# Reads of scratch and states moved to GpSimd's queue, with a new head, RMS step and end, in a one-core decoder layer

## The chip, the core and the metric

The kernel runs on one NeuronCore of a Trainium2 chip. Its engines work in parallel and meet through semaphores: TensorE (PE, matmuls; its weight loads are shown as PEld), VectorE (DVE), ScalarE (ACT), GpSimd (POOL) and SyncE (SP, which here only issues DMAs). Each engine takes its instructions strictly in order. A DMA is issued by an engine's queue and carried out by 16 shared DMA engines; SyncE and GpSimd issue them here. The metric is device time in microseconds (us); less is better.

## The reference

One inference step of one layer (DEPTH = 1), all in float32, for a prompt of 256 tokens and 8 samples of 8 tokens each (320 tokens, D_MODEL = 2048), with shared weights:

```
mod = silu(c) @ w_ada + b_ada                      # six vectors of 2048 per sequence: shift, scale, gate, twice
h   = rms_norm(x) * (1 + scale_m) + shift_m
z   = h @ w_in                                     # RWKV columns (3328), gMLP u, v (1024 each), gate logits (2 x 2048)
o_a = rwkv7(token_shift(z_rwkv), states)           # per head: S <- S diag(w) - (S kk)(a kk)^T + v k^T, in 16 heads of 64
y_a = o_a @ w_branch_a
y_b = (gelu(u) * (W_s @ layer_norm(gelu(v)) + b)) @ w_branch_b      # mixing in chunks of 128 positions
x   = x + gate_m * ((sigmoid(g_a) * y_a + sigmoid(g_b) * y_b) @ w_out)
h2  = rms_norm(x) * (1 + scale_f) + shift_f
x   = x + gate_f * ((silu(h2 @ w_gate) * (h2 @ w_up)) @ w_ffn_out)  # D_FF = 5632
y   = rms_norm(x)
```

Outputs are y of both groups, the new RWKV states and shift buffers of both, and the normalised gMLP v rows of the samples.

## The kernel before

The 320 tokens are the moving columns of every matmul and channels lie on partitions. A product in float32 is made of three matmuls with operands split into a high and a low part (`mms`, lines 174 to 176: high x high, low x high, high x low). Weights come as tiles `ws` of up to 1 MB (`wload`, line 162; `wf` in the FFN, line 1289) into three buffers; ScalarE copies the high part (`wh`) and VectorE subtracts it for the low part (`wl`), each in four buffers. So a weight tile is on the way, waits to be split, or is split, and TensorE works on the split parts in the order in which the program was written, as a scheduler placed it on each engine before the run.

The stages, in order of time:

- **Head** (0 to about 200 us). `x_stats` squares x in four quarters (two buffers `sq`), sums them with a matmul against ones (line 366) and takes root and reciprocal (`rst`). `ada_half` and `ada_cols` load columns of w_ada (tiles `wa`, lines 279 and 306) and multiply them with silu(c) (lines 281, 317); w_in's first 26 column tiles follow as soon as a stretch of h is modulated (`h_mod`), into `zx`.
- **Preparation** (about 200 to 400 us). Per pair of heads j, `prep1` to `prep3` build the recurrence's operands and store them in DRAM scratch: `d_w` (line 753), `d_kc` (754), `d_l` (763). The gate logits of w_in are worked off between them by `fill(n)`, which takes n units from a list of matmul units, and stored in `d_sg` (`g_evict`, line 548, four buffers `sg`).
- **Samples** (about 400 to 560 us). `chunk_load(4)` reads M, KB, v, Q and KC back (lines 824 to 843), `solve_load` reads the triangular systems (778, 780), `sample_t` the transposed states `s0t` (984, two buffers), `state_load` the states `s0` (971, three buffers) and the decays `dp` (1000). `sample_keys` has GpSimd and VectorE make the key products `we`; `sample_state` (line 1020) multiplies, adds and stores the new state (1022).
- **Prompt chunks** (about 560 to 750 us). Four chunks of 64 tokens, each with `chunk_load`, `chunk_g`, `chunk_w`, `chunk_t` (Tc and Lc, lines 884 and 889), `chunk_x`, `chunk_o`, `chunk_s` and `chunk_n` (factors `gb`, line 950; stores `d_o`).
- **Branches** (about 740 to 880 us). `read_split` (553) reads the two branch inputs back; w_branch_b and w_branch_a follow with their gate tiles `gt` read by `ahead_of` (562, six buffers of each kind). Branch b's gated result goes to `d_mb` (569) and is read again for branch a.
- **w_out and the RMS step** (about 880 to 1030 us). `o_evict` adds to the residual `xr` and sums squares in `acc`; `token_sums` (1236) makes sums per token, `rn2` the reciprocal roots, `dg` diagonals, and a matmul with ones (1266) spreads them to all partitions for h2 (`h2h`, `h2l`).
- **FFN** (about 1030 to 1975 us) and the **end**: the last RMS norm, a product with `rf` in seven parts (`y`), each part stored by SyncE (1356).

The modulation columns of groups 2 to 5 are a list `adas` of 17 units a group (16 loads of 1 MB, with a batch of 16 matmuls at every second one, and a flush). `fill` takes from it at a rate per unit until 17 are left, which are group 5's; the RMS step takes three of these and the FFN the rest.

All stores, the parameter rows and the residual's x are issued by GpSimd (`sd = nc.gpsimd.dma_start`); everything else, that is weights, modulation columns and all reads of scratch and states, by SyncE (`ld = nc.sync.dma_start`).

Of the kernel before, what the change touches and what calls it, by code (L numbers as in the profile page):

```python
# [42 lines left out]
F_C = [4, 2, 2, 3, 2, 3, 2, 2]  # L43
NIA, NB1, NB2 = 2, 1, 2
F_S = [1, 8, 2, 2, 6, 8, 2, 1]
# [29 lines left out]
def body(ctx, tc, I, O):  # L75
# [192 lines left out]
    def ada_half(k0, nk):  # L268

        w, kb, box = nk * 256, 8 // nk, {}  # L270

        def load(q):
            if q == 0:
                box["pa"] = ps_ax(512)
            a = 4 * q % kb
            if a == 0:
                box["wt"] = st.tile([128, kb, w], F32, tag="wa", name="wa", bufs=2)
            wt = box["wt"][:, a:a + 4]
            ld(wt, w_ada.block(4 * q, 4, (k0 * 128, nk * 128), (D + k0 * 128, nk * 128)))
# [18 lines left out]
        return [lambda q=q: load(q) for q in range(4)] + [flush]  # L298

    def ada_cols(pool, kb, c0s, w, dsts, kr=1, bufs=2):  # L300

        box, held = {}, []

        def load(kq):
            wt = (pool or late["w"])().tile([128, kb, 4 * w], F32, tag="wa", name="wa", bufs=bufs)
            ld(wt, w_ada.block(kq * kb, kb, *[(c0, 4 * w // len(c0s)) for c0 in c0s]))
            held.append((kq, wt))
# [23 lines left out]
    def ada_seg(k0, nk):  # L331
        if nk < 4:
            return ada_half(k0, nk)

        def dsts(pt):
            for gi in range(2):
                c = BADA + gi * KT + k0
                tt(mod[:, gi, k0:k0 + 4].rearrange("p (jj b) s -> p b jj s", b=2), pt[:, :, 2 * gi:2 * gi + 2, 0:9],
                   bct(par1[:, c:c + 4].rearrange("p (jj b) -> p b jj", b=2), 9), ADD)
            scale_of(amix, 1, GMIX, k0, 4)  # L340

        return ada_cols(lambda: st, 2, [k0 * 128, D + k0 * 128], 256, dsts)

# [49 lines left out]
    with tc.manual_schedule(engines={mybir.EngineType.Activation, mybir.EngineType.DVE, mybir.EngineType.PE}):  # L393
# [10 lines left out]
        rst2 = st.tile([128, T], F32, name="rst2")  # L404
        V.tensor_copy(rst2, rst)
    rst = rst2
    def rows2():
        sd(par2, I["par2"])
        sd(psh, I["state_shift"])


    units, avail = deque(), [SEGS[0][1]]
    for si, (k0, nk) in enumerate(SEGS[1:]):
# [11 lines left out]
        if si == 2:  # L425
            u.insert(0, params2)
        units.extend((f, RA[si]) for f in u)
# [340 lines left out]
    def solve_load():  # L768
# [49 lines left out]
    def chunk_load(c):  # L818
# [4 lines left out]
        for h, lo in ((0, 0), (1, 64)):  # L823
            ld(b["M"][lo:lo + 64, :, h], d_w[lo:lo + 64, c, :, 0:2].rearrange("p j q t -> p j (q t)"))
        ld(b["KB"][0:64], d_w[0:64, c, :, 2:4])
        for q in range(2):
            ld(b["KB"][64:128, :, q], d_w[64:128, c, :, 3 - q])

        for a in range(2):
            for h in range(2):  # L830
                ld(b["v"][64 * a:64 * a + 64, :, 1 - h], d_w[64 * h:64 * h + 64, c, a::2, 4])
        if c == 4:

            b["Q"] = cp.tile([128, NJ, 2, 2, 4, 2, TS], F32, name="Q2", tag="Q2")
            for a in range(2):
                for h in range(2):
                    ld(b["Q"][64 * a:64 * a + 64, :, h].rearrange("p j q a s t -> p j (q a s t)"), d_w[64 * h:64 * h + 64, 4, :, 0:2].rearrange("p j q t -> p j (q t)"))
# [3 lines left out]
            ld(b["KC"][0:64], d_kc[0:64])  # L841
            for q in range(2):
                ld(b["KC"][64:128, :, q], d_kc[64:128, :, 1 - q])
        cur[c] = b
# [36 lines left out]
    def chunk_t(c):  # L881
        b = cur[c]
        b["T"] = cp.tile([128, NJ, 64], F32, name="Tc", tag="Tc", bufs=nb)
        ld(b["T"], d_t[c].rearrange("j p t -> p j t"))
        if c == 4:
            return

        T, L = b["T"], cp.tile([128, NJ, 64], F32, name="Lc", tag="Lc", bufs=1)
        ld(L, d_l[c].rearrange("j p t -> p j t"))
        pt = ps_ax(NJ, 32)  # L890
# [78 lines left out]
    def load_s0(j):  # L969
        s0 = cm.tile([128, NS, 64], F32, name="s0", tag="s0", bufs=3)  # L970
        ld(s0, I["s0"][j])
        return s0
# [8 lines left out]
    def sample_t(j):  # L981

        s0t = cm.tile([128, 4, 128], F32, name="s0t", tag="s0t", bufs=2)
        ld(s0t, I["s0t"][j])
        return s0t
# [245 lines left out]
    def token_sums():  # L1231

        pn = ps_ax(3)
        for c, n in enumerate(rows):
            for q, a in enumerate((acc, fin["q"])):
                PE.matmul(pn[0:n, c:c + 1], a[:, c * 128:c * 128 + n], ones[:, 0:1], start=q == 0, stop=q == 1)
        return pn
# [17 lines left out]
    dg = p2.tile([128, T], F32, name="dg")  # L1255
# [4 lines left out]
    for c, n in enumerate(rows):  # L1260
        fin["d"] = V.tensor_scalar(dg[0:n, c * 128:c * 128 + n], ident[0:n, 0:n], rn2[0:n, c:c + 1], None, op0=MUL)
    for _ in range(NB2):
        adas.popleft()()
    rB = ps_ax(T)
    for c, n in enumerate(rows):
        PE.matmul(rB[:, c * 128:c * 128 + n], ones[0:n], dg[0:n, c * 128:c * 128 + n], start=True, stop=True)
    h2h = hp.tile([128, KT, T], F32R, name="h2h", tag="hh")
# [78 lines left out]

    pf = ps_ax(T)
    for q, a in enumerate((acc, fin["q"])):
        PE.matmul(pf, ones, a, start=q == 0, stop=q == 1)
    rf = p2.tile([128, T], F32, name="rf", tag="sq2", bufs=2)  # L1350
# [9 lines left out]
_OUTS = {"y": (128, KT, T), "wkv_p": (2, 64, NJ, 64), "shift": (128, 9, NRW), "wkv_s": (NJ, 128, NS, 64), "v": (NS * TS, 1024)}  # L1360

# [56 lines left out]
```

## Time and profile before

| | |
|---|---|
| time, median of 3 runs (lowest, highest) | 1992.02 us (1989.43, 1995.13) |
| profiled execution, its span | 1994.61 us, 1992.9 us |
| TensorE busy; mean granted clock | 1931.9 us (97%); 0.986 |
| VectorE, ScalarE, GpSimd busy | 1079.7, 763.2, 119.3 us |
| DMA moved | 420.89 MB, 211 GB/s over the span |

The span runs from the first to the last instruction of the profiled execution; its time has a little around it. Matmuls are pipelined and their ends are modelled, so a busy TensorE can still be at less than its best pace. A DMA-issuing instruction counts as busy time on GpSimd and not on SyncE.

### The profile page before, as it was taken

The page shows a single profiled execution, that of the slowest core. Times are in us where ns is not written, and L with a number is a line of the kernel's source. Part 1 is how long each engine was busy: PE and PEld are TensorE (multiplying, and loading weights), DVE is VectorE, ACT ScalarE, POOL GpSimd, SP SyncE. Part 2 cuts the span into 40 slices and gives each one's busy share as a digit, 9 for nine tenths or more (in the row PEclk, how much of TensorE's full clock was granted, in tenths as well). Part 3 has the DMA queues.
Part 4 walks back from the last instruction along what each step waited for, and adds up shares of the span by engine and source line. Part 5 has one row for each costly group of instructions (what it writes and reads, how often), then busy time and mean ns, then how long its engine had stood idle before and what let it go on. Part 6 is the DMA issues. An engine that isn't in the chain of part 4 may idle for free.

```text
span 1992.9 us, 34504 instructions
## 1 busy us (share of the span) xinstructions
PE 1931.9 (97%) x14213; PEld 1807.8 (91%) x14213; DVE 1079.7 (54%) x1902; ACT 763.2 (38%) x1095; POOL 119.3 (6%) x221
## 2 busy tenths in 40 slices
PE   6999999989999999899999999999999999999996
PEld 4788999979886898888889999999999999999996
DVE  5666677759655564464464335345454445345446
ACT  5333377534333334342244232333333333332333
POOL 1000112330310011000000000000000000000000
PEclk9999999989999999999989999999999999999998
DMA  7877446785798789888746753544535544453441
GB/s 295 312 303 302 153 157 253 258 212 188 218 259 267 236 322 317 301 308 346 296 166 221 258 180 117 159 159 142 164 129 159 159 159 130 153 173 127 149 169 74
DMA packets 132813, 420.89 MB, mean 211 GB/s; under 512 B 41872, under 2 KB 65424, under 8 KB 103728
## 3 DMA queue, kind: packets, MB, share of 16 engines
q1 hardware_dynamic: 124256, 388.19, 57.7%
q0 software_dynamic: 8400, 30.50, 4.3%
q8 instruction: 112, 1.84, 0.4%
q14 instruction: 45, 0.37, 0.1%
HBM read 390.40 MB, written 28.23 MB: 210 GB/s over the span
## 4 chain that ended last, share of the span: by engine, by line
PE 79%; issue 12%; DMA 3%; DVE 2%; POOL 2%; ACT 1%; SPq 0%; DVEq 0%; POOLq 0%; ACTq 0%
PE mm L174 25%; PE mm L175 24%; PE mm L176 24%; PE ax L317 2%; DMA gt<-d_sg 1%; PE ax L281 1%; DMA d_mb<-gt 1%; POOL d_sg L548 0%; DMA d_w<-pk 0%; DVE wl L98 0%; ACT wh L101 0%; DMA KB<-d_w 0%; DMA dp<-d_pe 0%; POOL we L98 0%; DMA par<-in_par 0%
## 5 line engine op out<-in xcount | busy, mean ns | idle before, releaser
L98 DVE TENSOR_TENSOR wl<-ws,wh 128x1024 fp32r<-128x1024 f32 (+1 forms) x304 | 362.4, 1212 | 284.8 <-ACT wh L101 284.5
L101 ACT ACTIVATE wh<-ws 128x1024 fp32r<-128x1024 f32 (+1 forms) x304 | 305.8, 1041 | 458.1 <-PE mm L175 346.7
L174 PE MATMUL mm<-h2h,wh 128*128 128x320 f32 x1408 | 436.4, 310 | 2.1 <-ACT h2h L101 2.1
L175 PE MATMUL mm<-h2l,wh 128*128 128x320 f32 x1408 | 435.9, 310 | 0.0
L176 PE MATMUL mm<-h2h,wl 128*128 128x320 f32 x1408 | 435.6, 310 | 0.0
L98 DVE TENSOR_TENSOR wl<-wf,wh 128x1024 fp32r<-128x1024 f32 x176 | 215.2, 1225 | 327.3 <-ACT wh L101 322.7
L174 PE MATMUL mm<-hh,wh 128*128 128x320 f32 x1184 | 376.9, 321 | 2.6 <-ACT wh L101 2.6
L176 PE MATMUL mm<-hh,wl 128*128 128x320 f32 x1184 | 369.4, 313 | 1.8 <-DVE wl L98 1.7
L175 PE MATMUL mm<-hl,wh 128*128 128x320 f32 x1184 | 370.2, 313 | 0.3 <-DVE hl L98 0.3
L101 ACT ACTIVATE wh<-wf 128x1024 fp32r<-128x1024 f32 x176 | 185.2, 1058 | 383.2 <-PE mm L175 358.2
L174 PEld LDWEIGHTS mm<-h2h,wh 128*128 128x128 f32 x1408 | 265.0, 188 | 8.1 <-issue 2.5
L175 PEld LDWEIGHTS mm<-h2l,wh 128*128 128x128 f32 x1408 | 265.1, 188 | 0.0
L176 PEld LDWEIGHTS mm<-h2h,wl 128*128 128x128 f32 x1408 | 265.0, 188 | 0.0
L174 PEld LDWEIGHTS mm<-hh,wh 128*128 128x128 f32 x1184 | 224.7, 191 | 28.1 <-issue 16.6
L175 PEld LDWEIGHTS mm<-hl,wh 128*128 128x128 f32 x1184 | 225.5, 190 | 6.1 <-issue 2.5
L176 PEld LDWEIGHTS mm<-hh,wl 128*128 128x128 f32 x1184 | 225.0, 190 | 6.1 <-DVE wl L98 3.4
L175 PE MATMUL mm<-fl,wh 128*128 128x320 f32 x704 | 216.5, 308 | 0.0
L174 PE MATMUL mm<-fh,wh 128*128 128x320 f32 x704 | 216.4, 307 | 0.0
L176 PE MATMUL mm<-fh,wl 128*128 128x320 f32 x704 | 216.3, 308 | 0.0
L176 PEld LDWEIGHTS mm<-fh,wl 128*128 128x128 f32 x704 | 131.9, 187 | 0.1
L174 PEld LDWEIGHTS mm<-fh,wh 128*128 128x128 f32 x704 | 131.9, 187 | 0.0
L175 PEld LDWEIGHTS mm<-fl,wh 128*128 128x128 f32 x704 | 131.9, 187 | 0.0
(322 smaller groups left out, 2144.5 us busy)
## 6 DMA issues: line engine op xcount, KB each, us to landing
wa<-in_w_ada SPq DMA_DIRECT2D x88, 1024.0 KB, 6.6
wf<-in_w_ffn_in SPq DMA_DIRECT2D x176, 512.0 KB, 3.5
ws<-in_w_in SPq DMA_DIRECT2D x64, 1024.0 KB, 6.6
ws<-in_w_ffn_out SPq DMA_DIRECT2D x40, 1024.0 KB, 4.8
ws<-in_w_out SPq DMA_DIRECT2D x16, 1024.0 KB, 7.1
d_w<-pk POOLq DMA_DIRECT2D x8, 1120.0 KB, 6.1
wa<-in_w_ada SPq DMA_DIRECT2D x16, 512.0 KB, 5.0
ws<-in_w_branch_b SPq DMA_DIRECT2D x8, 1024.0 KB, 6.1
```

Source lines behind the costliest of these rows:

```text
L98: return (eng or V).tensor_tensor(out, a, b, op=op)
L101: return A.activation(out, in_, fn, **kw)
L174: PE.matmul(ps, hi[:, k, sl], xh[:, kx + a + k], start=f, stop=False)
L175: PE.matmul(ps, hi[:, k, sl], xl[:, kx + a + k], start=False, stop=False)
L176: PE.matmul(ps, lo[:, k, sl], xh[:, kx + a + k], start=False, stop=e)
L281: PE.matmul(box["pa"][32 * j:32 * j + 32, 0:w], cT[:, 4 * q + j], wt[:, j], start=q == 0, stop=q == 3, tile_position=(0, 32 * j))
L317: PE.matmul(box["pa"][32 * j:32 * j + 32, 0:w], cT[:, k], wt[:, kk, j * w:j * w + w], start=kq == kr - 1 and q == kq and kk == 0, stop=kq ...
```

## The change

1. Reads of scratch and of recurrent states are issued by GpSimd: every `ld` of lines 553, 562, 778, 780, 824 to 843, 884, 889, 950, 971, 984 and 1000 becomes `sd`. SyncE keeps weights, modulation columns, the head's x and the final stores.
2. Head: the squares of x are written into `zx` (unused until then) in four places; the tiles `wa` get a third buffer; `params2` is put behind the head on VectorE.
3. RMS step: sums per token in three full groups of 128 (the last two overlap by 64 tokens) with one root and one reciprocal; a batch of group 5's modulation matmuls ahead of the sums, one between sums and spreading, one behind it. Its first four loads are issued by GpSimd during w_out, into buffers of the FFN that are still free.
4. End: sums per token as in the RMS step; y is turned on TensorE in 12 groups of four 128 x 128 transposes, scaled per token while it is copied out of PSUM by ScalarE and VectorE in turn, and stored in 12 parts with another layout of the output, which the host turns back.

```
-    sq = st.tile([128, 4, T], F32, name="sq", tag="sq", bufs=2)          # x_stats
+    sq = zx[:, 4 * q:4 * q + 4, 0:T]
-    box["wt"] = st.tile([128, kb, w], F32, tag="wa", name="wa", bufs=2)   # ada_half; ada_seg's ada_cols too
+    box["wt"] = st.tile([128, kb, w], F32, tag="wa", name="wa", bufs=3)
-        V.tensor_copy(rst2, rst)
+        headed = V.tensor_copy(rst2, rst)
+    def late_params2():
+        with tc.issue_after(headed.ins):
+            params2()
...
-            ld(um, src[:, j])                                             # read_split
+            sd(um, src[:, j])
-                ld(got[n, i], src[i])                                     # ahead_of
+                sd(got[n, i], src[i])
-            ld(b["M"][lo:lo + 64, :, h], d_w[lo:lo + 64, c, :, 0:2]...)   # chunk_load; KB, v, Q, KC likewise
+            sd(b["M"][lo:lo + 64, :, h], d_w[lo:lo + 64, c, :, 0:2]...)
...
+    def ada_ahead():
+        for kq in range(4):
+            t = p2.tile([128, FCH[0][1], T], F32R, name="wb", tag=("fh", "fl")[kq % 2], bufs=2)
+            wt = early[5 * D, kq] = t.rearrange(...)
+            sd(wt, w_ada.block(kq, 1, (5 * D, D)))                         # ada_cols' load takes it from early
...
+    fill(24)
+    ada_ahead()
     while main_q:
         fill(1)
-    while len(adas) > 15 + NB1:                                           # NB1 = 1
+    while len(adas) > 15:
         adas.popleft()()
     pn = token_sums()
-    for n, c0, c1 in ((128, 0, 2), (64, 2, 3)):
-        fin["a"] = act(rn2[0:n, c0:c1], pn[0:n, c0:c1], AF.Sqrt, scale=1.0 / D, bias=eps6[0:n])
-        V.reciprocal(rn2[0:n, c0:c1], rn2[0:n, c0:c1])
+    fin["a"] = act(rn2, pn, AF.Sqrt, scale=1.0 / D, bias=eps6)
+    V.reciprocal(rn2, rn2)
...                                                                        # dg, then two units of adas, as before
     rB = ps_ax(T)
-        PE.matmul(rB[:, c * 128:c * 128 + n], ones[0:n], dg[0:n, c * 128:c * 128 + n], start=True, stop=True)
+        PE.matmul(rB[:, t0:t0 + 128], ones, dg[:, c], start=True, stop=True)
+    for _ in range(2):
+        adas.popleft()()
...
-    act(rf, pf, AF.Sqrt, scale=1.0 / D, bias=eps6)                        # the end
-    V.reciprocal(rf, rf)
-    for k0, nk, eng in ((0, 1, V), (11, 2, G), (1, 2, V), (3, 2, V), (5, 3, V), (13, 3, G), (8, 3, V)):
-        o = y[:, k0:k0 + nk]
-        tt(o, o, rf.unsqueeze(1).to_broadcast([128, nk, T]), MUL, eng)
-        ld(O["y"][:, k0:k0 + nk], o)
+    def turned(c, q):
+        pt = ps_ax(4, 128)
+        t0 = (0, 128, T - 128)[c]
+        for k in range(4):
+            PE.transpose(pt[:, k], y[:, 4 * q + k, t0:t0 + 128], ident)
+        return pt.rearrange("p k t -> p (k t)")
+    first = [(0, 0), (0, 1), (0, 2)]
+    ahead = [turned(*cq) for cq in first]
+    pf = token_sums()
...
+    for n, (c, q) in enumerate(first + [(1, 0), (1, 1), (1, 2), (0, 3), (1, 3)] + [(2, q) for q in range(4)]):
+        pt = ahead[n] if n < len(ahead) else turned(c, q)
+        p0 = 64 if c == 2 else 0
+        o = ...
+        if n % 2:
+            V.tensor_scalar(o, pt[p0:], rf[p0:, c:c + 1], None, op0=MUL)
+        else:
+            act(o, pt[p0:], AF.Copy, scale=rf[p0:, c:c + 1])
+        ld(O["y"][c, q, 0:128 - p0], o)
```

## Rows read from the trace of the kernel before

**Rows 1.** Busy us (instructions) of PE, PEld, DVE, ACT, POOL; PEclk, DMA share, GB/s, by stretch.

```profile
404.00:416.00 12.00, 7.32 (x36) 6.75 (x34) 3.70 (x2) 1.84 (x2) 7.03 (x16) 0.72 1.11 237
436.00:450.00 14.00, 9.19 (x75) 8.50 (x74) 10.82 (x33) 4.01 (x4) 4.25 (x8) 0.76 0.83 292
524.00:560.00 36.00, 33.94 (x248) 25.67 (x247) 26.91 (x43) 10.59 (x15) 13.38 (x18) 0.98 0.74 238
560.00:750.00 190.00, 183.94 (x1959) 157.18 (x1958) 105.18 (x127) 68.68 (x103) 13.87 (x22) 0.98 0.85 270
750.00:875.00 125.00, 117.60 (x802) 105.88 (x801) 59.21 (x91) 51.51 (x85) 10.22 (x19) 1.00 0.87 311
1019.00:1034.00 15.00, 11.56 (x59) 8.72 (x58) 10.19 (x33) 6.94 (x15) 0.00 (x0) 0.66 0.56 200
```

**Rows 2.** Waits of TensorE: engine, line, released by: total us, times, longest.

```profile
PE mm L174 <- DVE gt L98: 4.8, 3, 2.8
PE ax L858 <- DMA KB<-d_w: 4.7, 1, 4.7
PE ax L992 <- DMA s0t<-in_s0t: 3.1, 1, 3.1
```

**Rows 3.** SyncE's queue in order of time, 390 to 436 us: start, us, instruction.

```profile
391.57 0.33 SPq L162 DMA_DIRECT2D ws<-in_w_in  x1
...
433.08 0.38 SPq L162 DMA_DIRECT2D ws<-in_w_in  x1
```

**Rows 4.** DMA issues of lines 548, 753 and 824: ns min/median/max, first and last start.

```profile
L548 POOL DMA_DIRECT2D d_sg<-sg x32: 542/542/708, 278.8 to 753.2; - x32
...
L753 POOL DMA_DIRECT2D d_w<-pk x8: 836/868/875, 298.1 to 393.5; - x8
...
L824 SPq DMA_DIRECT2D M<-d_w x10: 579/629/1619, 402.7 to 655.3; - x10
```

**Rows 5.** GpSimd's groups, 524 to 560 us: busy us, mean ns, idle before.

```profile
L98 POOL TENSOR_TENSOR we<-Wt,bm 128x512 f32<-128x512 f32 x6 | 6.8, 1130 | 18.0 <-PE ax L1020 18.0
L1022 POOL DMA_DIRECT2D out_wkv_s<-s x8 | 4.5, 567 | 6.5 <-DVE um L98 2.7 <-PE ax L1020 2.0 <-DVE s L98 1.7
```

**Rows 6.** The head in order of time, all engines.

```profile
3.86 1.98 SPq L279 DMA_DIRECT2D wa<-in_w_ada  x4
...
12.56 2.58 ACT L101 ACTIVATE sq<-xt 128x1280 f32<-128x1280 f32 x2 [4.50 <-PE ax L366]
...
18.00 2.70 PE L281 MATMUL ax<-wa,cT 128*32 128x256 f32 x32
...
25.96 1.44 PE L174 MATMUL mm<-hh,wh 128*128 128x320 f32 x4
```

**Rows 7.** Line 279's eight issues from 0 to 26 us, issue to landing.

```profile
DMA to landing us min/median/max: 3.7/7.3/10.6
```

**Rows 8.** The RMS step in order of time, all engines.

```profile
1020.74 0.38 PE L1236 MATMUL ax<-ones,acc 128*128 128x1 f32 x2 [1.37 <-DVE acc L98]
...
1022.04 2.62 PE L317 MATMUL ax<-wa,cT 128*32 128x512 f32 x16
...
1022.67 0.62 DVE L1261 TENSOR_SCALAR dg<-ident,rn 128x128 f32<-128x128 f32 x3
...
1028.50 0.90 PE L174 MATMUL mm<-h2h,wh 128*128 128x320 f32 x2 [2.06 <-ACT h2h L101]
```

**Rows 9.** The chain that ended last, in order of time: start, us, what.

```profile
1066.15 1.85 PE ax L317 x16
```

**Rows 10.** The end in order of time, all engines.

```profile
1976.66 0.81 PE L1349 MATMUL ax<-sq,ones 128*128 128x320 f32 x2 [0.99 <-ACT sq L101]
...
1980.25 7.45 DVE L98 TENSOR_TENSOR y<-y,rf 128x320 f32<-128x320 f32 x5
...
1980.77 7.44 SPq L1356 DMA_DIRECT2D out_y<-y  x7
```

**Rows 11.** TensorE in order of time, 584 to 592 us.

```profile
586.50 0.63 PE L872 MATMUL ax<-ident,KB 128*128 128x128 f32 x4 [0.21 <-DVE Dt L98]
```

More of the change, by code (lines that the diff above doesn't have):

```diff
@@ L43 @@
 F_C = [4, 2, 2, 3, 2, 3, 2, 2]
-NIA, NB1, NB2 = 2, 1, 2
+NIA = 2
 F_S = [1, 8, 2, 2, 6, 8, 2, 1]
@@ L298, in ada_half @@
         return [lambda q=q: load(q) for q in range(4)] + [flush]
+    early = {}
     def ada_cols(pool, kb, c0s, w, dsts, kr=1, bufs=2):
@@ L304, in load @@
         def load(kq):
-            wt = (pool or late["w"])().tile([128, kb, 4 * w], F32, tag="wa", name="wa", bufs=bufs)
-            ld(wt, w_ada.block(kq * kb, kb, *[(c0, 4 * w // len(c0s)) for c0 in c0s]))
+            wt = early.pop((c0s[0], kq), None)
+            if wt is None:
+                wt = (pool or late["w"])().tile([128, kb, 4 * w], F32, tag="wa", name="wa", bufs=bufs)
+                ld(wt, w_ada.block(kq * kb, kb, *[(c0, 4 * w // len(c0s)) for c0 in c0s]))
             held.append((kq, wt))
@@ L425, in body @@
         if si == 2:
-            u.insert(0, params2)
+            u.insert(0, late_params2)
         units.extend((f, RA[si]) for f in u)
@@ L823, in chunk_load @@
         for h, lo in ((0, 0), (1, 64)):
-            ld(b["M"][lo:lo + 64, :, h], d_w[lo:lo + 64, c, :, 0:2].rearrange("p j q t -> p j (q t)"))
-        ld(b["KB"][0:64], d_w[0:64, c, :, 2:4])
+            sd(b["M"][lo:lo + 64, :, h], d_w[lo:lo + 64, c, :, 0:2].rearrange("p j q t -> p j (q t)"))
+        sd(b["KB"][0:64], d_w[0:64, c, :, 2:4])
         for q in range(2):
-            ld(b["KB"][64:128, :, q], d_w[64:128, c, :, 3 - q])
+            sd(b["KB"][64:128, :, q], d_w[64:128, c, :, 3 - q])
         for a in range(2):
             for h in range(2):
-                ld(b["v"][64 * a:64 * a + 64, :, 1 - h], d_w[64 * h:64 * h + 64, c, a::2, 4])
+                sd(b["v"][64 * a:64 * a + 64, :, 1 - h], d_w[64 * h:64 * h + 64, c, a::2, 4])
         if c == 4:
@@ L840, in chunk_load @@
             b["KC"] = cp.tile([128, NJ, 2, 64], F32, name="KC", tag="KC")
-            ld(b["KC"][0:64], d_kc[0:64])
+            sd(b["KC"][0:64], d_kc[0:64])
             for q in range(2):
-                ld(b["KC"][64:128, :, q], d_kc[64:128, :, 1 - q])
+                sd(b["KC"][64:128, :, q], d_kc[64:128, :, 1 - q])
         cur[c] = b
@@ L883, in chunk_t @@
         b["T"] = cp.tile([128, NJ, 64], F32, name="Tc", tag="Tc", bufs=nb)
-        ld(b["T"], d_t[c].rearrange("j p t -> p j t"))
+        sd(b["T"], d_t[c].rearrange("j p t -> p j t"))
         if c == 4:
@@ L949, in chunk_n @@
         gb = cp.tile([128, NJ, 2, 64], F32, name="ggc", tag="we")
-        ld(gb, d_w[:, c, :, 5:7])
+        sd(gb, d_w[:, c, :, 5:7])
         pc_ = ps_ax(512)
@@ L970, in load_s0 @@
         s0 = cm.tile([128, NS, 64], F32, name="s0", tag="s0", bufs=3)
-        ld(s0, I["s0"][j])
+        sd(s0, I["s0"][j])
         return s0
@@ L983, in sample_t @@
         s0t = cm.tile([128, 4, 128], F32, name="s0t", tag="s0t", bufs=2)
-        ld(s0t, I["s0t"][j])
+        sd(s0t, I["s0t"][j])
         return s0t
@@ L1233, in token_sums @@
         pn = ps_ax(3)
-        for c, n in enumerate(rows):
+        for c, t0 in enumerate((0, 128, T - 128)):
             for q, a in enumerate((acc, fin["q"])):
-                PE.matmul(pn[0:n, c:c + 1], a[:, c * 128:c * 128 + n], ones[:, 0:1], start=q == 0, stop=q == 1)
+                PE.matmul(pn[:, c:c + 1], a[:, t0:t0 + 128], ones[:, 0:1], start=q == 0, stop=q == 1)
         return pn
@@ L1248, in body @@
     main_q.extend(group_units(I["w_out"], KT, mh, ml, groups(0, 16), o_evict))
+    fill(24)
+    ada_ahead()
     while main_q:
         fill(1)
-    while len(adas) > 15 + NB1:
+    while len(adas) > 15:
         adas.popleft()()
     rn2 = p2.tile([128, 3], F32, name="rn2")
-    dg = p2.tile([128, T], F32, name="dg")
+    dg = p2.tile([128, 3, 128], F32, name="dg")
     pn = token_sums()
-    for n, c0, c1 in ((128, 0, 2), (64, 2, 3)):
-        fin["a"] = act(rn2[0:n, c0:c1], pn[0:n, c0:c1], AF.Sqrt, scale=1.0 / D, bias=eps6[0:n])
-        V.reciprocal(rn2[0:n, c0:c1], rn2[0:n, c0:c1])
-    for c, n in enumerate(rows):
-        fin["d"] = V.tensor_scalar(dg[0:n, c * 128:c * 128 + n], ident[0:n, 0:n], rn2[0:n, c:c + 1], None, op0=MUL)
-    for _ in range(NB2):
+    fin["a"] = act(rn2, pn, AF.Sqrt, scale=1.0 / D, bias=eps6)
+    V.reciprocal(rn2, rn2)
+    for c, t0 in enumerate((0, 128, T - 128)):
+        fin["d"] = V.tensor_scalar(dg[:, c], ident, rn2[:, c:c + 1], None, op0=MUL)
+    for _ in range(2):
         adas.popleft()()
     rB = ps_ax(T)
-    for c, n in enumerate(rows):
-        PE.matmul(rB[:, c * 128:c * 128 + n], ones[0:n], dg[0:n, c * 128:c * 128 + n], start=True, stop=True)
+    for c, t0 in enumerate((0, 128, T - 128)):
+        PE.matmul(rB[:, t0:t0 + 128], ones, dg[:, c], start=True, stop=True)
+    for _ in range(2):
+        adas.popleft()()
     h2h = hp.tile([128, KT, T], F32R, name="h2h", tag="hh")
@@ L1344, in body @@
         f()
[L1347 to L1350, printed above, removed]
-    act(rf, pf, AF.Sqrt, scale=1.0 / D, bias=eps6)
-    V.reciprocal(rf, rf)
-    for k0, nk, eng in ((0, 1, V), (11, 2, G), (1, 2, V), (3, 2, V), (5, 3, V), (13, 3, G), (8, 3, V)):
-        o = y[:, k0:k0 + nk]
-        tt(o, o, rf.unsqueeze(1).to_broadcast([128, nk, T]), MUL, eng)
-        ld(O["y"][:, k0:k0 + nk], o)
+    def turned(c, q):
[7 more added lines that the diff above has]
+    pf = token_sums()
+    rf = p2.tile([128, 4], F32, name="rf")
+    act(rf[:, 0:2], pf[:, 0:2], AF.Sqrt, scale=1.0 / D, bias=eps6)
+    act(rf[64:128, 2:3], pf[64:128, 2:3], AF.Sqrt, scale=1.0 / D, bias=eps6[64:128])
+    V.reciprocal(rf[:, 0:2], rf[:, 0:2])
+    V.reciprocal(rf[64:128, 2:3], rf[64:128, 2:3])
+    yt = [hp.tile([128, 8, 512], F32, name="yt", tag="hl"), p2.tile([128, 8, T], F32, name="yu", tag="fl", bufs=2)]
+    for n, (c, q) in enumerate(first + [(1, 0), (1, 1), (1, 2), (0, 3), (1, 3)] + [(2, q) for q in range(4)]):
+        pt = ahead[n] if n < len(ahead) else turned(c, q)
+        p0 = 64 if c == 2 else 0
+        o = yt[0][p0:, n] if n < 8 else yt[1].rearrange("p a t -> p (a t)")[p0:, q * 512:q * 512 + 512]
+        if n % 2:
[3 more added lines that the diff above has]
+        ld(O["y"][c, q, 0:128 - p0], o)
 _PACKED = ["w_ada", "w_in", "w_branch_a", "w_branch_b", "w_out", "w_ffn_in", "w_ffn_out"]
-_OUTS = {"y": (128, KT, T), "wkv_p": (2, 64, NJ, 64), "shift": (128, 9, NRW), "wkv_s": (NJ, 128, NS, 64), "v": (NS * TS, 1024)}
+_OUTS = {"y": (3, 4, 128, 512), "wkv_p": (2, 64, NJ, 64), "shift": (128, 9, NRW), "wkv_s": (NJ, 128, NS, 64), "v": (NS * TS, 1024)}
 def laid_out(a):
```

15 lines of the change are left out of this document (8 added, 7 removed).

## The prediction

> **What bounds the kernel now.** I read the busy times of the engines by stretch first, then TensorE's waits, then SyncE's own queue, then the order of time around each edit. TensorE is the bound: it is busy for nearly all of the span, so the change can only win where TensorE idles or runs at the lower of its two clock levels, or where work leaves its queue. The reader should see six such places. Idle time is the length of a stretch less TensorE's busy time; the share of the clock that was not granted, times the length, bounds what the lower level cost. From 404 to 416 us TensorE idles 4.7 us with 0.72 of its clock granted, from 436 to 450 it idles 4.8 us with 0.76, from 524 to 560 2.1 us, from 560 to 750 6.1 us with 0.98 (3.8 us more), from 750 to 875 7.4 us at full clock, and from 1019 to 1034 3.4 us with 0.66 [rows 1]. The largest waits name what was late: the mask-and-multiply of a gate tile (4.8 us), the chunk's keys KB (4.7 us), a recurrent state s0t (3.1 us) [rows 2]. All three end in reads that the change moves. Last, SyncE's queue: between 391.57 and 433.08 us it issues no weight, because 28 scratch and state reads stand there, the first of them waiting for its data [rows 3].
>
> The two other places are the head, before dense matmuls start, and the end, where nothing but the last norm runs.
>
> **Part 1, the reads.** 172 reads leave SyncE for GpSimd, counted from the loops: 64 of branch and gate tiles (lines 553, 562), 52 of a chunk's operands (M 10, KB 15, v 20, Q 4, KC 3), 10 for the solve, 9 for T and L, 5 for the norm's factors, 32 for the sample states (s0t 8, s0 8, dp 16). GpSimd's issue takes 0.54 us for a store of plain rows and 0.87 us for one cut into many short runs; on SyncE the M reads, cut the same way, take 0.63 us [rows 4]. So 172 reads cost GpSimd 93 us (at 0.54) to 150 us (at 0.87), spread over some 470 us in which it is mostly idle. I take 0.63, the row of the same read: 108 us. That alone hides; what does not is where GpSimd is already in the chain.
>
> Place by place, gains negative.
>
> From 404 to 416 us: GpSimd is busy 7.0 of these 12 us [rows 1] and now also issues M and KB; two or three of its clears come first. KB lands 1 to 2 us later, and weights now run beside it. +2 (0 to +4), since nothing covers this wait today.
>
> From 436 to 450 us: The weights that were held from 391.57 to 433.08 [rows 3] are issued when their buffers come free, so the wait on a split weight goes, and if the state arrives too, the 4.8 us and 0.24 x 14 = 3.4 us of lost clock go: 0 to -8. s0t(2) still needs the buffer of s0t(0), as now, so half: -4.
>
> From 524 to 560 us: Per pair of heads (j) GpSimd has one key product of 1.13 us and one store of 0.57 [rows 5]; three reads of 0.63 come on top, 1.9 us each pair. Eight pairs: 15 us. Today there is 36 - 13.4 = 22.6 us of idle GpSimd [rows 1], so it fits on average, but stores, key products and reads now queue behind one another and the states' DVE products wait for the reads. +3 (-2 to +10).
>
> From 560 to 750 us: Weights no longer wait behind blocked reads; stores of gate logits queue behind reads that wait for their buffers instead. 6.1 us idle and 3.8 us of clock are there to win: -2 (-8 to +5).
>
> From 750 to 875 us: The gate reads wait for stores of d_mb to land, and hold the weights behind them today. -4 of the 7.4 us (0 to -7).
>
> Sum of part 1: -5, with -14 to +7 if the places are taken as independent (roots of the summed squares of their distances).
>
> What speaks against the move: a store of gate logits from GpSimd takes 0.54 us at the median and 0.71 us at most in 32 issues [rows 4], with VectorE busy for 105 of the 190 us from 560 on [rows 1]. The Trainium skill (SBUF — State Buffer, section "Summary: rules for kernel authors") advises against hiding a GpSimd-issued DMA under VectorE work, because a two-port VectorE mode keeps GpSimd from writing its descriptors. By that rule reads would come late wherever VectorE is busy; the stores of this trace do not show it. It is rival 3. The second point is rate: what I count on is that weights no longer stand behind a waiting read [rows 3], not faster transfers. The Trainium skill (DMA: Bandwidth & Descriptors, section "Issuing engines are not separate DMA queues") says that issuing from several engines saves only the time of issuing. By that rule part 1 would be 0, which is the near edge of rival 1.
>
> **Part 2, the head.** The squares of x now go to zx, four places in place of two, so the third square doesn't wait for TensorE: it began at 12.56 us after 4.50 us of idle that ended with TensorE, not with a landing [rows 6]. Eleven small VectorE instructions leave this chain. But the modulation weights bound it next: the fourth issue of the first group starts at about 5.4 us and lands 10.6 us later, at 16.0 [rows 6, 7]. Their 32 matmuls ran from 18.00 to 20.70 [rows 6]; with three of four tiles already worked on, they can end near 17 us. From there to the first dense matmul it was 5.3 us (25.96 - 20.70), in which the second group's loads were waited for; the third buffer lets those go out earlier. So -3.7 from the landing alone, up to -5.5 if the second group is no longer waited for. I take -4 (-2.5 to -5.5). After 26 us TensorE is dense, so a start that is earlier is kept unless weights are late; the third buffer speaks against that.
>
> **Part 3, the RMS step at 1020 us.** Sums of columns start at 1020.74 after 1.37 us of waiting, the 16 modulation matmuls at 1022.04 take 2.62, the broadcast takes until 1026.44 (1028.50 less the 2.06 of waiting), then TensorE waits 2.06 us for the first h2h [rows 8]. The change puts one more batch before the sums and one behind the broadcast. A batch is 1.85 us at full clock and sits in the FFN's path [rows 9]. Two batches move into waits of 1.37 and 2.06 us: the first overhangs by 0.5 us, the second fits: 2 x 1.85 - 0.5 = 3.2 saved. One root in place of two and full clock for batch and broadcast save about 1 us. If the clock stays at 2.4 GHz, up to 0.34 x 15 = 5.1 us less the 3.4 idle [rows 1], some 2 us, come on top. Of 4.2 to 6.2 saved I take -5.5 (-3 to -7). ada_ahead's four reads of 1 MB go out beside w_out's weights, where TensorE does not idle; up to +2 if they slow them, 0 taken.
>
> **Part 4, the end.** From the last sum at 1976.66 to the first product at 1980.25 it is 3.6 us [rows 10]. The new sums are 12 one-column matmuls, 1.30 us (1020.74 to 1022.04), and root and reciprocal of few columns, 0.63 us (to 1022.67) [rows 8]: 1.9 us, 1.7 less. Then the products of 7.45 us [rows 10] are replaced by 9 groups of 4 transposes at 0.16 us (4 in 0.63) [rows 11], 5.7 us, and 12 scaled copies shared by two engines. At 2.1 ns a column (7.45 us for 3520) a copy of 512 takes 1.1, six of them 6.5 us. So the last store is issued at about 1978.6 + 6.5 = 1985 instead of 1988.2 [rows 10], but the same 2.6 MB must leave, and its first part goes only 1 us earlier. -2 (-3 to -1). If TensorE falls to 1.2 GHz the transposes take 11.3 us and the end is 3 us later than now.
>
> **The sum.** -5 -4 -5.5 -2 = -16.5. The profiled execution took 1994.6 us (span 1992.9, 1.7 around it): 1978.1. It lay 2.6 us above the median of the three runs; against that median, 1992.0, it is 1975.5, and I say 1976.
>
> **Rivals.** The first: The reads give nothing (0 to +9): GpSimd's waits cost as much as SyncE's gave. For it: 404 to 416 us gets worse and only there is the wait sure. Against it: [rows 3]. 1992.0 - 11.5 + (0 to 9): 1980.5 to 1989.5.
>
> The second is slower: GpSimd's line becomes the bound in the sample states (524 to 560 us) and the gate stages. There a store of d_sg or s0 stands behind a read that waits; four gate buffers fill, ScalarE stops in its queue, and with it the split of the weights. It decides once a pair of heads takes GpSimd longer than the 4.5 us that the stretch now gives it (36 / 8; 1.13 + 0.57 + 1.9 = 3.6 without waits), that is, when waits add more than 0.9 us a pair. With 3 us more a pair, 24, one drop of the clock as at 436 us, 3.4, and the -8 of the other places, part 1 is +19 and the total 1992.0 - 11.5 + 19 = 2000. For it: 9 us of slack in 36 are little, and in-order queues lose more than their sum. Against it: the state's reads need nothing that is late today.
>
> The third: GpSimd is kept from writing descriptors by VectorE: each read is late by one VectorE instruction. The nearest row of an instruction on that side is the 1.13 us key product [rows 5]; half of it, times VectorE's busy share of 0.55 [rows 1], is 0.31 us a read, 53 us in all; if TensorE sees a third of it, as an estimate, part 1 is -5 + 18 and the total 1993. Against it: the 0.54 us of [rows 4].
>
> The fourth: All of what is idle from 404 to 875 comes back: part 1 is -15 to -25 (idle time of 25 us and the lost clock stand there, [rows 1]), 1955 to 1966. Against it: the wait for KB stays.
>
> **How the numbers follow.** Chances: forecast (1966 to 1980.5) 0.50; rival 1 0.21; rival 2 0.12; rival 3 0.04; rival 4 0.13. A measurement can tell 0.3%, 6 us, from no change: faster is under 1986, slower over 1998. Rival 1 is split at 1986, 0.10 to 0.11; of rival 2, 0.03 end within 6 us; rival 3 is half same and half slower: faster 0.50 + 0.13 + 0.10 = 0.73, same 0.11 + 0.03 + 0.02 = 0.16, slower 0.09 + 0.02 = 0.11. The range leaves out rivals 2 and 3 and the far part of 4: 1961 to 1990; the likeliest case's own is 1966 to 1980.5.
>
> **What would show it.** Right: SyncE issues weights between 392 and 433 us; the gate-tile waits of [rows 2] are gone; dense matmuls start by 22 us; three modulation batches stand around the RMS step with the clock granted; the last store goes out before 1988 less what came before. Wrong: TensorE waits on key products, s0 or dp; ScalarE idles for a gate buffer; GpSimd is busy without a gap over 524 to 560 us; the transposes run at half clock. The prediction falls if part 1 comes out over +5.

## The result, and the profile after

The change made the kernel slower: 2018.78 us at the median of 4 runs (2013.98 to 2024.8) against 1990.72 us for the kernel before (4 runs), a ratio of 1.0151 with an interval of 1.0132 to 1.0170. The profiled execution took 2021.24 us, its span 2019.5 us, 26.6 us more than the 1992.9 of before. The forecast was 1976 us, with a range of 1961 to 1990.

Where the time went is read from landmarks, the same matmuls in both traces, each taken to 0.1 us. The measured column is the difference after less before; the forecast column has the prediction's term.

| from, to | before, us | after, us | measured | forecast |
|---|---|---|---|---|
| start, last matmul of the preparation | 390.3 | 385.3 | -5.0 | -4 |
| to the first matmul on KB | 20.9 | 22.9 | +2.0 | +2 |
| to the first branch matmul | 341.6 | 342.9 | +1.3 | -3 |
| to the first matmul of w_out | 134.5 | 171.1 | **+36.6** | **-4** |
| to the last matmul of w_out | 131.8 | 132.6 | +0.8 | 0 |
| to the last matmul of the FFN | 955.7 | 949.2 | -6.5 | -5.5 |
| to the end of the span | 18.1 | 15.5 | -2.6 | -2 |

One stage lost it all. Windows of after, with the columns of [rows 1]; the branch stages are later and longer now and stand in two windows:

```profile
404.00:416.00 12.00, 7.83 (x45) 7.30 (x47) 1.80 (x2) 2.70 (x3) 3.98 (x6) 0.72 1.04 212
436.00:450.00 14.00, 14.00 (x130) 13.23 (x129) 8.01 (x36) 4.13 (x4) 7.05 (x19) 1.00 0.72 239
524.00:560.00 36.00, 35.24 (x217) 28.50 (x216) 27.33 (x36) 7.99 (x10) 24.66 (x33) 1.00 0.71 213
560.00:750.00 190.00, 178.19 (x1914) 150.93 (x1916) 106.84 (x133) 70.61 (x106) 57.39 (x87) 0.96 0.87 270
750.00:842.00 92.00, 70.59 (x444) 63.00 (x436) 28.41 (x40) 27.99 (x46) 21.54 (x40) 0.87 0.64 227
842.00:922.00 80.00, 69.06 (x432) 62.58 (x432) 39.54 (x65) 28.60 (x45) 15.05 (x28) 0.91 0.71 263
```

From 436 to 450 us TensorE is now busy throughout at full clock: the forecast gain is there. Part of it is lost again at once, in a stretch that had no term. These are 74 us of before and, 3 us earlier like its landmark, the same stretch of after; idle time grows from 0.5 to 3.8 us:

```profile
453.00:527.00 74.00, 73.54 (x660) 69.46 (x658) 61.25 (x112) 31.71 (x48) 10.07 (x13) 1.00 0.62 190
```

```profile
450.00:524.00 74.00, 70.21 (x616) 65.82 (x614) 59.69 (x125) 28.31 (x44) 20.76 (x32) 0.98 0.60 197
```

From 524 to 560 us GpSimd is busy for 24.7 of 36 us, and TensorE idles less than before. From 560 to 750 us TensorE idles 11.8 us where it idled 6.1, and from 750 to 922 us it idles 32.3 us, with part of its clock gone as well.

TensorE's waits of after, answering to [rows 2] (waiting instruction, what released it: total us, times, longest):

```profile
PE mm L174 <- ACT wh L101: 25.2, 5, 9.2
...
PE ax L866 <- DMA KB<-d_w: 8.7, 2, 4.4
PE mm L174 <- ACT oh L101: 6.0, 1, 6.0
...
PE mm L174 <- DVE gt L98: 0.7, 2, 0.5
```

The wait for gate products (4.8 us) is nearly gone, as forecast, and one five times as long stands in its place: TensorE waits for ScalarE's split of weights. Before, that wait was short:

```profile
PE mm L174 <- ACT wh L101: 2.9, 3, 2.4
```

The weights themselves had been there. In the branch stages SyncE, which now issues only weights and modulation columns, waits for a weight buffer to be emptied by the split: 31.0 us in before (753 to 887 us) and 144.9 in after (751 to 922 us):

```profile
SPq L162 <- DVE wl L98: 144.9, 16, 20.3
```

SyncE's queue from 390 to 436 us shows that its part came true; where [rows 3] has no weight between 391.57 and 433.08 us, five go out:

```profile
395.26 40.50 SPq L162 DMA_DIRECT2D ws<-in_w_in  x5
```

What ScalarE waited for in the branch stages, from 751 to 922 us of after:

```profile
ACT gt L101 <- DMA gt<-d_sg: 90.7, 24, 13.8
...
ACT wh L101 <- PE mm L175: 2.1, 2, 1.4
```

and from 753 to 887 us of before:

```profile
ACT gt L101 <- DMA gt<-d_sg: 57.7, 16, 9.4
...
ACT wh L101 <- PE mm L175: 5.7, 4, 2.4
```

ScalarE waits 33 us longer for gate tiles. Its waits for TensorE to give a buffer of split weights back, a sign that the split is ahead, fall from 5.7 to 2.1 us. The gate reads themselves (line 562, now 570), their duration, and the longest that GpSimd waited for ahead of them:

```profile
L570 POOL DMA_DIRECT2D gt<-d_sg x32: 539/542/650, 737.1 to 909.1; - x32
...
  DMA d_mb<-gt: 38.2, 10
```

The landings were waited for before as well, and nearly as long, but by SyncE (line 562), while GpSimd's stores of d_mb waited for nothing but VectorE's products. Both lines are of before, from 740 to 930 us:

```profile
SPq L562 <- DMA d_mb<-gt: 34.0, 6, 12.0
```

```profile
POOL d_mb L569 <- DVE gt L98: 59.7, 8, 17.1
```

So the change did not make the wait; it moved the wait ahead of the stores that end it. The mechanism is in 30 us of the order of time, in picked lines of GpSimd, VectorE, ScalarE and TensorE:

```profile
771.58 0.55 POOL L577 DMA_DIRECT2D d_mb<-gt  x1 [2.67 <-DVE gt L98]
772.80 0.88 DVE L98 TENSOR_TENSOR gt<-gt,mm 128x320 f32<-128x320 f32 x2
777.40 0.54 POOL L570 DMA_DIRECT2D gt<-d_sg  x1 [4.08 <-DMA d_mb<-gt]
777.94 0.54 POOL L577 DMA_DIRECT2D d_mb<-gt  x1
782.99 0.47 ACT L101 ACTIVATE gt<-gt 128x320 f32<-128x320 f32 x1 [9.71 <-DMA gt<-d_sg]
784.59 0.54 POOL L570 DMA_DIRECT2D gt<-d_sg  x1 [3.97 <-DMA d_mb<-gt]
...
794.98 0.47 ACT L101 ACTIVATE gt<-gt 128x320 f32<-128x320 f32 x1 [3.29 <-DMA gt<-d_sg]
795.36 3.88 ACT L101 ACTIVATE wh<-ws 128x1024 fp32r<-128x1024 f32 x4
799.33 0.60 PE L174 MATMUL mm<-umhl,wh 128*128 128x320 f32 x1 [9.21 <-ACT wh L101]
```

The gate read at 777.40 needs the buffer that the store of 771.58 empties, so it waits for that store to land. The products of 772.80 were done by 773.7, but their stores stand behind the waiting read; the first goes out at 777.94, and the read at 784.59 waits for its landing in turn. Each round is store, landing, read, landing. ScalarE's next sigmoids want these tiles, and four splits of weights are queued behind the sigmoids. TensorE stands still for 9.21 us.

The other parts, answering to [rows 6, 8, 10]: first dense matmul, the three modulation batches and the first h2h, transposes and stores.

```profile
21.88 0.82 PE L174 MATMUL mm<-hh,wh 128*128 128x320 f32 x4 [0.48 <-DVE hh L389]
...
1055.03 1.92 PE L321 MATMUL ax<-wb,cT 128*32 128x512 f32 x16
1058.31 1.92 PE L321 MATMUL ax<-wb,cT 128*32 128x512 f32 x16
1061.03 1.92 PE L321 MATMUL ax<-wa,cT 128*32 128x512 f32 x16
1063.95 0.85 PE L174 MATMUL mm<-h2h,wh 128*128 128x320 f32 x4 [1.00 <-ACT h2h L101]
...
2007.71 6.09 PE L1370 MATMUL ax<-ident,y 128*128 128x128 f32 x36 [0.63 <-ACT rf L101]
...
2014.31 2.47 SPq L1390 DMA_DIRECT2D out_y<-yu  x4
```

Around the RMS step the clock is granted in full, where it was 0.66 [rows 1]:

```profile
1052.00:1068.00 16.00, 15.00 (x115) 10.29 (x114) 11.32 (x35) 8.94 (x17) 0.00 (x0) 1.00 0.47 154
```

### The profile page after: what moved, and what is told of

Read it like the earlier page. It is cut to its first block, busy times and chain, and to the rows that moved or that the text cites. A ratio compares the mean times of both kernels' runs of the same rounds, so it can differ in the third digit from the quotient of the medians.

```text
span 2019.5 us, 34610 instructions
## 1 busy us (share of the span) xinstructions
PE 1946.7 (96%) x14269; PEld 1824.4 (90%) x14269; DVE 1072.8 (53%) x1903; ACT 767.9 (38%) x1101; POOL 223.3 (11%) x395
## 4 chain that ended last, share of the span: by engine, by line
PE 82%; DMA 8%; issue 4%; DVE 2%; POOL 2%; ACT 1%; SPq 0%; POOLq 0%; ACTq 0%; DVEq 0%
PE mm L174 25%; PE mm L175 24%; PE mm L176 24%; PE ax L321 3%; DMA d_mb<-gt 2%; DMA wa<-in_w_ada 2%; DMA gt<-d_sg 1%; DMA KB<-d_w 1%; PE ax L281 1%; ACT wh L101 1%; POOL gt L570 1%; DMA um<-d_o 0%; DMA xt<-in_x 0%; DMA Tc<-d_t 0%; DVE wl L98 0%
```

## The experiments

The theory after this reading is a loop in GpSimd's queue (store, landing, read, next store). Twelve kernels were run. Each ratio is against the kernel before, timed on the same chip (1989.4 to 1991.8 us), with its interval.

### Parts 2 to 4 alone, and with the reads up to 750 us

The first kernel is the changed one with every moved read back on SyncE; the second has only the branch stages' reads back.

```
-            sd(um, src[:, j])                  # second kernel: these two lines alone
+            ld(um, src[:, j])
-                sd(got[n, i], src[i])
+                ld(got[n, i], src[i])
```

> The changed kernel with every moved read back on SyncE, so parts 2 to 4 alone. By the landmarks of the two traces the head gives 5.0 us, the RMS step 6.3 and the end 2.6: 1990.7 - 13.9 = 1977 us (1974 to 1980). By the prediction's terms, 11.5 us: 1979. If the reads up to 750 us cost 3.3 us, as the same landmarks say, this kernel is 3 us faster than the one with only the branch reads back on SyncE; if they give 1 us, as the prediction's terms for 404 to 750 us sum to, 1 us slower. Rival (earlier weights of part 1 carried part of these gains): over 1984.

> The changed kernel with the branch inputs um and the gate tiles gt read by SyncE again (64 of the 172 reads); the other reads stay on GpSimd. Theory (a loop in GpSimd's queue: a store of d_mb stands behind the read of a later gate tile, and that read waits for the landing of an earlier store of d_mb; ScalarE waits at the gate's sigmoid with the splits of the weights behind it): the branch stages go back from 171 us to the 134.5 us of the kernel before, so 2018.8 - 36.6 = 1982 us (1978 to 1988). Rival (the loss is spread over all the reads that GpSimd issues, and only shows where TensorE has little else to do): half of it stays, over 1995 us.

Parts 2 to 4: 1977.88 us, 0.9926 (0.9904 to 0.9947). With the reads up to 750 us on GpSimd too: 1978.79 us, 0.9933 (0.9912 to 0.9954). So parts 2 to 4 gave 12.4 us of medians, 108 reads moved without the branches give nothing that can be told (nor can the 3 us of loss and the 1 us of gain that were weighed be told apart), and the branch stages' 64 reads cost 40 us. What is won from 430 to 445 us is lost behind it, mostly in the prompt's chunks. Windows of the second kernel:

```profile
430.00:445.00 15.00, 15.00 (x115) 14.70 (x115) 7.64 (x24) 6.04 (x6) 7.07 (x18) 1.00 0.73 244
...
560.00:749.00 189.00, 176.47 (x1904) 147.50 (x1903) 103.51 (x127) 70.50 (x109) 49.38 (x73) 0.96 0.86 267
```

and of the first:

```profile
430.00:445.00 15.00, 10.06 (x81) 9.68 (x82) 13.44 (x37) 4.02 (x5) 4.23 (x8) 0.77 0.76 256
...
560.00:749.00 189.00, 182.95 (x1970) 155.52 (x1969) 101.14 (x125) 71.81 (x112) 15.44 (x25) 0.99 0.87 276
```

### The gate reads alone

The kernel before with one line changed (562: `ld` becomes `sd`).

> The kernel before with one edit: the 48 reads of gate tiles (line 562) issued by GpSimd. Theory (loop in GpSimd's queue): this alone brings the loss, 1990.7 + 30 to 40 = 2021 to 2031 us. Rival (the loss is spread over all 172 reads): 48 of 172 of it or less, under 2002 us.

2022.87 us, 1.0149 (1.0120 to 1.0179): +32.6 us from 48 reads. A loss spread over all reads is out. TensorE's largest wait is the one of after:

```profile
PE mm L174 <- ACT wh L101: 25.9, 6, 8.8
```

### Opening the loop

```
         act(sg, sg, AF.Sigmoid)
-        tt(sg, sg, ps, MUL)
-        sd(d_mb[i], sg)
+        tt(mb := ob.tile([128, T], F32, name="mb", tag="mb", bufs=4), sg, ps, MUL)
+        sd(d_mb[i], mb)
...
-                sd(got[n, i], src[i])                   # the second kernel in addition
+                (ld if n else sd)(got[n, i], src[i])    # n = 1: d_mb
```

> The changed kernel with all reads on GpSimd, but branch b's gated result in a tile of its own (mb, four buffers), so that a gate tile's buffer is free once VectorE has multiplied, and the read of the next gate tile does not wait for a store to land. Theory (loop of store, landing and read in one queue): most of the 36.6 us goes, 1982 to 1994 us, and GpSimd no longer waits for d_mb ahead of reads of d_sg. Rival (GpSimd is too slow or too late as an issuer of 64 more reads, whatever they wait for): little changes, 2009 to 2019 us.

> The changed kernel with branch b's result in a tile of its own, as in the run before with that edit (1996.3 us), and the 16 reads of d_mb issued by SyncE; reads of d_sg and stores of d_mb stay on GpSimd. Theory (what was left there comes from reads of d_mb that wait for a landing and have gate reads and stores behind them): 1979 to 1987 us. Rival (what was left comes from stores that wait for VectorE's product and have gate reads behind them): 1992 to 2000.

1996.31 us, 1.0027 (1.0011 to 1.0044): 22.5 of the 40 us are gone, a little short of the range. With the reads of d_mb on SyncE: 1983.95 us, 0.9972 (0.9956 to 0.9989), as the theory had it. So reads that wait for a landing with other reads and stores behind them make most of it, and GpSimd as an issuer of the other 32 gate reads makes little. In the first of the two, GpSimd's gate reads wait for landings 9.0 us in place of 38.2:

```profile
  DMA d_mb<-mb: 9.0, 3
```

### More buffers

`NGT = 6` becomes `NGT = 8`.

> The changed kernel with one size changed: eight gate tiles of each kind in place of six. TensorE, VectorE and SyncE have the same order of instructions; GpSimd and ScalarE nearly. Theory (a gate read waits for the landing of a store that stands little ahead of it): with two whole groups of four tiles, that store lies a group further back, and half or more of the 36.6 us goes: 1984 to 2000 us. Rival (ScalarE's order, four sigmoids ahead of four splits, makes the loss by itself): 2010 to 2019.

2017.78 us, 1.0144 (1.0114 to 1.0175): the theory missed, and the time lies in the rival's range. The gate reads still wait for landings, and ScalarE for them:

```profile
  DMA d_mb<-gt: 34.8, 11
...
  ACT gt L101: 87.0, 23
```

With two more buffers each read, and each sigmoid, was placed two tiles earlier, as soon as a buffer could be free by the plan. The tile that ScalarE waits for is then wanted later by its product, but the sigmoid stands ahead of the same splits. The theory from here has two parts: the loop makes tiles late, and ScalarE's order passes that on to TensorE.

### ScalarE's order

The sigmoid is queued behind the splits of its own group's weights, in both branches. The orders of TensorE and SyncE stay, VectorE's and GpSimd's nearly: where reads are on GpSimd, a store of d_mb goes ahead of two reads of d_o and another changes places with a read of d_mb.

```
-        act(hi, s, AF.Copy)                                             # wsplit
+        kept["wh"] = act(hi, s, AF.Copy)
...
-        act(sg, sg, AF.Sigmoid)                                         # yb_evict, ya_evict
+        with tc.issue_after(kept["wh"].ins): act(sg, sg, AF.Sigmoid)
```

> The changed kernel with one order changed: ScalarE gets the sigmoid of a gate tile behind the splits of the weights of that tile's own group of four, in both branches. GpSimd's queue keeps its order of stores and gate reads in the branches, and TensorE, VectorE and SyncE theirs. Theory as the run with eight tiles left it (two things together: GpSimd's loop makes gate tiles late, and ScalarE's early sigmoids pass that on to the weights): GpSimd still waits some 35 us for landings of d_mb, but half or more of the 36.6 us goes, 1984 to 2000 us. Rival (the loop alone: late gate tiles reach TensorE through PSUM buffers that wait for VectorE's products, whatever ScalarE's order): 2008 to 2019.

> Parts 2 to 4 with all reads on SyncE (1977.9 us) and the same single change of ScalarE's order: sigmoids behind the splits of their own group. All other engines keep their order. It completes the square of reads on GpSimd or SyncE by early or late sigmoids. Theory (early sigmoids cost only what the gate tiles are late, and with SyncE's reads that is little): the 4 to 6 us that TensorE idles in the branch stages go in part, 1972 to 1977 us. Rival (early sigmoids cost some 29 us wherever the reads are issued): under 1960 us. Third (late sigmoids hold PSUM buffers, so that the order costs as much as it gives): 1978 to 1983.

| median, us | sigmoids early | behind the splits |
|---|---|---|
| reads on SyncE (parts 2 to 4) | 1977.9 | 1970.5 |
| reads on GpSimd (parts 1 to 4) | 2018.8 | 1989.4 |

The ratios of the right column are 0.9903 (0.9876 to 0.9930) and 0.9997 (0.9979 to 1.0014). The order alone is worth 29.4 us where gate tiles are late, and 7.4 where reads are on SyncE, a little over the theory's range. Read down the columns, the reads on GpSimd cost 40.9 us with early sigmoids and still 18.9 with late ones: the loop and ScalarE's order together make 22 of the 41 us, and the other 19 reach TensorE with either order. In the kernel with reads on GpSimd and the new order, GpSimd still waits for landings from 740 to 930 us, longer than before the edit:

```profile
POOL gt L570 <- DMA d_mb<-gt: 47.3, 10, 6.8
```

but ScalarE's waits from 745 to 890 us are again those of the kernel before (57.7 and 5.7 us):

```profile
ACT gt L101 <- DMA gt<-d_sg: 54.5, 14, 10.9
...
ACT wh L101 <- PE mm L175: 5.6, 3, 2.4
```

TensorE's wait for split weights falls from 25.2 to 7.0 us, and a wait for VectorE's gate products, the way that the rival named, has 5.3:

```profile
PE mm L174 <- ACT wh L101: 7.0, 3, 4.9
PE mm L174 <- DVE gt L98: 5.3, 2, 5.0
```

### No stores of d_mb at all

Branch b's product stays in SBUF.

```
-        tt(sg, sg, ps, MUL)
-        sd(d_mb[i], sg)
+        kept[i] = ob.tile([128, T], F32, name="mb", tag="mb", bufs=16)
+        tt(kept[i], sg, ps, MUL)
...
-        sg, mb = got.pop((0, i)), got.pop((1, i))
+        sg, mb = got.pop((0, i)), kept.pop(i)
```

> The changed kernel with all its reads on GpSimd, and branch b's gated result kept in 16 tiles of SBUF: no store and no read of d_mb (um in two buffers and gate tiles in five, for room). Theory (only stores of d_mb and reads that wait for their landing, in one queue, cost time): 1976 to 1985 us, although 32 gate tiles and 16 branch inputs are still read by GpSimd. Rival (GpSimd is late as an issuer of gate reads, whatever they wait for): at least half of the loss stays, over 1998.

> Parts 2 to 4 with all reads on SyncE, and branch b's gated result kept in 16 tiles of SBUF, so that neither the 16 stores nor the 16 reads of d_mb are left (um in two buffers and gate tiles in five, for room). Theory (the wait of reads for landings of d_mb holds SyncE's weights a little in the kernel before too): the 4 us that TensorE idles in the branch stages of the kernel with parts 2 to 4 go, 1977.9 - 4 = 1974 us (1970 to 1976). Rival (that idle time is hidden or has other causes): within 2 us of 1977.9.

On GpSimd 1985.66 us, 0.9980 (0.9962 to 0.9998); on SyncE 1969.78 us, 0.9902 (0.9881 to 0.9923). The first is just above its range, the second just below: 8.1 us were won there, where 4 were expected. With d_mb gone, the reads on GpSimd cost 15.9 us (1985.66 less 1969.78) in place of 40.9. So most of the loss goes with the stores and reads of d_mb, but not all: from the first branch matmul to the first of w_out it takes 136.2 us against 126.9 on SyncE. Which read is late there was not taken further. On SyncE TensorE is busy for nearly the whole stage:

```profile
743.00:870.00 127.00, 125.90 (x867) 115.01 (x863) 68.73 (x105) 53.70 (x86) 0.54 (x1) 1.00 0.84 301
```

### Sample reads on GpSimd in that kernel

`sd if c == 4 else ld` in `chunk_load`, and `sd` in `solve_load` and `sample_t`; the second kernel adds s0, dp and the samples' Tc and factors.

> The fastest kernel so far (parts 2 to 4, branch b's result kept in SBUF, all reads on SyncE: 1969.8 us) with the reads of the samples' chunk, of the triangular systems and of s0t on GpSimd; reads of the prompt's chunks, gates, s0 and dp stay on SyncE. Theory (from 430 to 445 us the move gives 4 us of idle time and 5 us of lost clock, and what it gave was paid back at the prompt's chunks, where KB and a factor come late): 1962 to 1967 us. Rival (what is won there is given back a stage later whichever reads move): 1968 to 1973.

> The same with the reads of s0, dp, and the samples' Tc and factors on GpSimd too. Theory (these reads queue behind key products and stores of states there, but need nothing that is late): within 2 us of the run before. Rival (GpSimd's line is full from 524 to 560 us, as the prediction's second rival has it): 3 us or more slower than the run before.

1973.44 us, 0.9918 (0.9902 to 0.9933), and 1969.04 us, 0.9893 (0.9878 to 0.9909). The first theory missed, and the time is just above its rival's range too: what is won from 430 to 445 us comes back as a loss later with this choice of reads as well. In the second run the expectation was within 2 us of the first; it is 4 us faster, for a reason that was not looked for, and can't be told from the kernel without moved reads. GpSimd is busy for 22 of the 36 us from 524 on, and TensorE idles 0.6 us:

```profile
524.00:560.00 36.00, 35.36 (x222) 29.67 (x221) 27.51 (x40) 11.92 (x15) 22.04 (x30) 1.00 0.85 265
```

Three kernels lie at 1969 to 1970.5 us, 1% below the kernel before: b's product kept in SBUF, the same with the sample reads on GpSimd, and the new order of ScalarE. Two of these edits together were not run.

## Why the prediction was wrong

Parts 2, 3 and 4 came out as worked. Their terms sum to -11.5; the run of them alone gave -12.4. The squares in zx and the third buffer bring the first dense matmul from 25.96 to 21.88 us, and the start was kept. The RMS step has the three batches, the clock is granted, and the wait for h2h is 1.0 us in place of 2.06 [rows 8]. At the end the 36 later transposes take 0.17 us each, as taken.

Part 1 was forecast at -5 and is +40.9 (2018.8 less 1977.9). The prediction set +5 as the mark at which it falls.

**The step that failed** is the term for 750 to 875 us: "The gate reads wait for stores of d_mb to land, and hold the weights behind them today. -4 of the 7.4 us (0 to -7)." The wait was seen, and that it leaves SyncE. Not followed was where it goes: the stores for whose landing it waits are issued by the same GpSimd, so the next store is held by the read that the last one releases. And the term had no bound on the side of a loss. The wait itself is as long as before, 38.2 us on GpSimd against 34.0 on SyncE; what stands behind it is new. A wait that moves to another queue had to be costed with what is queued there, as it was for the other places. The opened loop gives 22.5 us back, or 34.8 with the reads of d_mb moved as well.

**The second rival had the shape and not the place.** It has a store behind a waiting read, and ScalarE stopped with the splits behind it. But it took stores of d_sg and s0, decided by GpSimd's time per pair of heads, and priced +19. From 524 to 560 us, where it should decide, TensorE idles 0.8 us in after against 2.1 [rows 1]. ScalarE did not stop for a gate buffer to store from but for a gate tile to arrive. Nor had the prediction looked at ScalarE's order of sigmoids and splits: with late sigmoids the move of the reads costs 18.9 us in place of 40.9.

The smaller places: 404 to 416 us was right (+2.0). From 436 to 450 us the far end of the range came, 8 us. From 450 to 524 us nothing was forecast, and 3.3 us of idle time and 1.5 of clock were lost. From 560 to 750 us -2 was taken; idle time grew by 5.7 us and 3.8 us more of clock were lost, beyond the range's worse end of +5. TensorE's longest wait there is for KB of a prompt's chunk (4.4 us). The places up to 750 us were forecast at -1 together, and by the medians of the two runs with the branches' reads on SyncE they made +0.9: near, but by luck, since the misses cancel. The prediction's list of TensorE's largest waits also passed over the largest of all, 12.6 us for the squares of x in the head, which part 2 worked on from other rows; it is 9.4 us in after.

The third rival, descriptors kept back by VectorE, shows nowhere: GpSimd's 32 reads of d_sg took 0.54 us at the median and 0.65 at most, and from issue to landing the gate reads took 4.9 us at the median, as on SyncE before. The Trainium skill (SBUF — State Buffer, section "Summary: rules for kernel authors") has a DMA from GpSimd starved while VectorE is in its 2x or 4x mode, not whenever VectorE is busy, as the prediction read it. From 751 to 922 us VectorE runs nothing but products, sums and differences of two tensors, in a mode that no row names, so these runs don't test that rule. By the Trainium skill's other rule (DMA: Bandwidth & Descriptors, section "Issuing engines are not separate DMA queues") issuing from more engines saves only issuing time. The 108 reads that gave nothing agree with it; it doesn't speak of the loss.

## What to carry to other kernels

Before a read moves to another queue, ask which store frees its buffer and on which queue that store is: read and store in one in-order queue make a chain of store, landing, read, landing for every tile, and two more buffers did not open it here, where reads are placed as early as they can be. Give the stored result a tile of its own, keep it in SBUF, or leave the read elsewhere. On an engine that also prepares the bound engine's operands, small work that waits for a transfer belongs behind that preparation: here it was worth 7 us with reads on SyncE and 29 where the loop made them late.

## What the runs showed that was not expected

TensorE pays for such waits twice. After the wait of 6.03 us that ends at 771.43 us, half the clock is granted (1.2 of 2.4 GHz): matmuls start 0.27 us apart, where it is 0.15 at full clock; after the wait that ends at 799.33 us likewise. Matmuls in a row, behind the first of these waits and later at full clock:

```profile
771.43 0.60 PE L174 MATMUL mm<-umhl,wh 128*128 128x320 f32 x1 [6.03 <-ACT oh L101]
771.83 0.47 PE L175 MATMUL mm<-umhl,wh 128*128 128x320 f32 x1
772.10 0.47 PE L176 MATMUL mm<-umhl,wl 128*128 128x320 f32 x1
...
778.23 0.31 PE L175 MATMUL mm<-umhl,wh 128*128 128x320 f32 x1
778.38 0.31 PE L176 MATMUL mm<-umhl,wl 128*128 128x320 f32 x1
```

With 0.87 and 0.91 of the clock granted in the two windows of the branch stages, up to 19 us of full-speed work (0.13 x 92 and 0.09 x 80) are missing beside 32.3 us of idle time.

A read of M, 0.63 us on SyncE [rows 4], took GpSimd 0.70, so the nearest row was a little low; GpSimd's busy time grew by 104 us for an estimated 108.
